# One projection moved from a mixture-of-experts routing phase into an attention phase, three routing sums in another number format, and weight splits issued in turns with gathered pieces

## The chip, the cores and the metric

The program runs on one core of a Trainium2 chip. A time is the device time of one execution of the whole program in microseconds (us); runs are compared by their median. The profiler gives the busy time of each engine: TensorE (PE; its weight loads are the separate row PEld), VectorE (DVE), ScalarE (ACT), GpSimd (POOL), and SyncE (SP), which only issues DMAs here. "Granted clock" (PEclk) is the share of TensorE's full clock that the chip granted: 1.00 is 2.4 GHz, 0.50 is 1.2 GHz.

## The reference

Two transformer blocks in float32 over T = 256 tokens of width D = 1024. The first block: causal attention, a convolutional feed-forward layer, a sliding-window attention with sinks (the "second attention" below), and again a feed-forward layer. The second block, cut to what matters here:

```python
def second_block(x, p, ...):
    h = _gdn_mixer(x, ...)                                  # gated delta net
    x = _layernorm(DEEPNORM_ALPHA * x + h, ln_g[i, 0], ln_b[i, 0])
    h = _hier_moe(x, ...)
    x = _layernorm(DEEPNORM_ALPHA * x + h, ln_g[i, 1], ln_b[i, 1])
    return x + sigmoid(x @ pe_w_gate[i]) * (p[i] @ pe_w_proj[i])   # p: 256 x 256

def _hier_moe(x, ...):                     # 4 groups of 8 experts
    g_logits = xt @ w_group + b_group
    g_onehot = one_hot(argmax(g_logits), 4)
    g_prob = sum(softmax(g_logits) * g_onehot, -1)
    e_logits = einsum("tge,tg->te", xt @ w_router + b_router, g_onehot)
    top_val, top_idx = top_k(e_logits, 2)
    top_w = softmax(top_val) * g_prob[:, None]
    # each expert: silu(xt @ w_gate) * (xt @ w_up), weighted, @ w_down
```

The product of `p` and `pe_w_proj` needs nothing of `x`, so it can be computed anywhere before the last line.

## The kernel before

Most weights are split into two halves: ScalarE rounds a piece of the loaded `raw` to fp32r (`whi`, L204), VectorE subtracts that from `raw` and keeps the rest (`wlo`, L207), and TensorE adds three products for each block, high by high, high by low and low by high (L217 to L219; for the experts L1350 to L1352). Some products are plain fp32 (L262, and p's), which the trace shows as two records each. Products of a projection go to PSUM tiles named `acc`.

The second attention (L770 on) runs over four chunks c of the query projection, each followed by softmax and attention for two pairs of heads: mask and scores (L445 to L449), maxima on VectorE (L451), exponentials on ScalarE (L463, into `pr`), transposes of the probabilities (L489), products with the values (L497).

The second block's mixture of experts has two phases. `d1` is the routing. `token_norm` makes the 36 logits `lg` (4 of groups, 32 of experts) from products that were formed along with the delta net's output projection (`rt`), the mean and rsqrt of the variance. `tokens` transposes x to token-major (`xtr`, `xt`) and makes its high half `xth` and the full normalized `xt`; `tokens_low` the low half `xtl`. `route` makes the one-hot group `g1h`, sums it over tokens on TensorE (`pp`, L1232 to L1236, with constant matrices `below` and `ones`), and from it the place of each token in its group (`key`); `put` makes the 0/1 matrices `kept` that sort tokens by group. `by_slot` gathers the sorted tokens with products (`ga`, L1291) and makes high and low halves of eight pieces (`xgh` on ScalarE L1304; `full` L1306 and `xgl` L1307 on VectorE); half 0 serves the first two groups. `over` looks whether a group has too many tokens (`ov`, the last reader of `pp`) and `weigh` computes the weights of the top two experts (up to `wi`). `side` is p's projection: 32 records `ppp` (L1432) in fp32, copied by ScalarE to `kept` tiles (L1433), which stay until the last line of the block.

`d2` runs over 4 groups of 8 experts. For each expert there are 24 products of gate and up (`gu`), an activation and a gate (`sg`, L1356, L1357, with the combining weight `cb`), a transposition (`htr`, L1363) and the down products (`y`, L1379 to L1381). Parts of other work run between them (`aside`: the combining weights `cbp` and `cb`, layer norm, the gather's second half).

Loads go through SyncE's queue into a ring of eight `raw` tiles in the second block (three in the attention phase); five pairs of `whi` and `wlo` hold split pieces of 1024 columns, four pieces being one expert's gate and up. Pools give a buffer out again when its last reader is done. The order on each engine is made by a scheduler; `behind(...)` says that instructions are issued after a given one. Each engine runs its list in order.

## Time and profile before

| | us |
|---|---|
| median of 3 runs (lowest and highest) | 1313.37 (1313.19 to 1313.55) |
| profiled execution | 1312.89 |
| its span | 1311.1 |
| TensorE busy | 1278.9 (98%) |
| VectorE busy | 1019.1 (78%) |
| ScalarE busy | 790.2 (60%) |

All times in this text are on the axis of the profiled execution's span, which begins at 0. The second attention's four chunks lie between 343.5 and 399, the routing phase between about 961 and 982, the experts behind it until 1240.

A line of the timeline names the start, the duration, the engine, the source line, what is written from what, the shape, and in brackets the time for which the engine stood idle ahead of it and what it waited for. Lines of source are those of the kernel before.

### The profile page before, as it was taken

The page shows a single profiled execution, that of the slowest core. Times are in us where ns is not written, and L with a number is a line of the kernel's source. Part 1 is how long each engine was busy: PE and PEld are TensorE (multiplying, and loading weights), DVE is VectorE, ACT ScalarE, POOL GpSimd, SP SyncE. Part 2 cuts the span into 40 slices and gives each one's busy share as a digit, 9 for nine tenths or more (in the row PEclk, how much of TensorE's full clock was granted, in tenths as well). Part 3 has the DMA queues.
Part 4 walks back from the last instruction along what each step waited for, and adds up shares of the span by engine and source line. Part 5 has one row for each costly group of instructions (what it writes and reads, how often), then busy time and mean ns, then how long its engine had stood idle before and what let it go on. Part 6 is the DMA issues. An engine that isn't in the chain of part 4 may idle for free.

```text
span 1311.1 us, 26079 instructions
## 1 busy us (share of the span) xinstructions
PE 1278.9 (98%) x10092; PEld 1149.3 (88%) x10092; DVE 1019.1 (78%) x2215; ACT 790.2 (60%) x1628; POOL 28.5 (2%) x51
## 2 busy tenths in 40 slices
PE   7999999999999999999999999999999999999998
PEld 7888999999879999999888787888987888888877
DVE  6677989866788988755766888666368899999985
ACT  6555667755556677653434464644257887878763
POOL 1000000000000010000100000000000000000000
PEclk9999999999999999999999999999989999999999
DMA  7434555555423555662254323243437999999951
GB/s 285 143 101 139 180 187 176 177 190 177 156 97 130 173 193 184 225 215 79 97 152 126 100 60 102 66 134 99 170 130 288 360 340 354 365 358 376 347 192 35
DMA packets 69570, 244.50 MB, mean 186 GB/s; under 512 B 24128, under 2 KB 26176, under 8 KB 45632
## 3 DMA queue, kind: packets, MB, share of 16 engines
q1 hardware_dynamic: 68288, 241.26, 52.9%
q8 instruction: 81, 1.33, 0.4%
q10 hardware_dynamic: 1152, 1.51, 0.4%
q14 instruction: 49, 0.40, 0.1%
HBM read 240.12 MB, written 2.62 MB: 185 GB/s over the span
## 4 chain that ended last, share of the span: by engine, by line
PE 86%; DVE 9%; ACT 2%; issue 1%; DMA 1%; SPq 0%; DVEq 0%; ACTq 0%
PE acc L217 11%; PE acc L218 11%; PE acc L219 11%; PE acc L292 10%; PE gu L1351 4%; PE gu L1350 4%; PE gu L1352 4%; PE acc L262 4%; PE y L1379 2%; PE y L1380 2%; PE y L1381 2%; PE acc L1614 2%; PE o L1164 2%; DVE wlo L207 1%; PE sc L489 1%
## 5 line engine op out<-in xcount | busy, mean ns | idle before, releaser
L207 DVE TENSOR_TENSOR wlo<-raw,whi 128x512 fp32r<-128x512 f32 (+1 forms) x542 | 467.8, 878 | 102.4 <-ACT whi L204 98.2
L204 ACT ACTIVATE whi<-raw 128x512 fp32r<-128x512 f32 (+1 forms) x542 | 418.1, 780 | 191.9 <-PE acc L218 132.7
L217 PE MATMUL acc<-xh,whi 128*128 128x256 f32 x892 | 258.0, 290 | 0.0
L219 PE MATMUL acc<-xh,wlo 128*128 128x256 f32 x892 | 252.0, 283 | 0.0
L218 PE MATMUL acc<-xl,whi 128*128 128x256 f32 x892 | 251.0, 282 | 0.0
L219 PEld LDWEIGHTS acc<-xh,wlo 128*128 128x128 f32 x892 | 169.8, 190 | 2.5 <-issue 2.5
L217 PEld LDWEIGHTS acc<-xh,whi 128*128 128x128 f32 x892 | 167.7, 188 | 3.0 <-issue 1.5
L218 PEld LDWEIGHTS acc<-xl,whi 128*128 128x128 f32 x892 | 168.0, 188 | 2.5 <-issue 1.5
L292 PE MATMUL acc<-x,raw 128*128 128x256 f32 x640 | 154.0, 386 | 0.4 <-issue 0.4
L292 PEld LDWEIGHTS acc<-x,raw 128*128 128x128 f32 x640 | 116.4, 190 | 15.0 <-issue 0.8
L1351 PE MATMUL gu<-wlo,xgh 128*128 128x512 f32 x256 | 103.7, 405 | 0.0
L1352 PE MATMUL gu<-whi,xgl 128*128 128x512 f32 x256 | 101.0, 394 | 1.7 <-DVE xgl L1307 1.6
L1350 PE MATMUL gu<-whi,xgh 128*128 128x512 f32 x256 | 101.3, 396 | 0.0
L219 PE MATMUL acc<-hh,wlo 128*128 128x256 f32 x352 | 99.6, 283 | 0.0
L218 PE MATMUL acc<-hl,whi 128*128 128x256 f32 x352 | 99.6, 283 | 0.0
L217 PE MATMUL acc<-hh,whi 128*128 128x256 f32 x352 | 99.6, 283 | 0.0
L262 PE MATMUL acc<-xf,raw 128*128 128x256 f32 x296 | 71.3, 379 | 0.0
L217 PEld LDWEIGHTS acc<-hh,whi 128*128 128x128 f32 x352 | 67.6, 192 | 0.0
L219 PEld LDWEIGHTS acc<-hh,wlo 128*128 128x128 f32 x352 | 67.6, 192 | 0.0
L218 PEld LDWEIGHTS acc<-hl,whi 128*128 128x128 f32 x352 | 67.6, 192 | 0.0
L1352 PEld LDWEIGHTS gu<-whi,xgl 128*128 128x128 f32 x256 | 48.6, 190 | 12.2 <-DVE xgl L1307 3.4
L262 PEld LDWEIGHTS acc<-xf,raw 128*128 128x128 f32 x296 | 52.9, 190 | 5.6 <-issue 0.2
(423 smaller groups left out, 2290.4 us busy)
## 6 DMA issues: line engine op xcount, KB each, us to landing
raw<-w_gu SPq DMA_DIRECT2D x64, 1024.0 KB, 7.3
raw<-w_up SPq DMA_DIRECT2D x44, 1024.0 KB, 4.8
raw<-w_ed SPq DMA_DIRECT2D x32, 1024.0 KB, 7.2
raw<-w_gin SPq DMA_DIRECT2D x96, 256.0 KB, 3.3
raw<-w_down SPq DMA_DIRECT2D x16, 1024.0 KB, 4.9
raw<-w_qk SPq DMA_DIRECT2D x8, 1024.0 KB, 5.0
raw<-w_gout SPq DMA_DIRECT2D x32, 256.0 KB, 2.9
raw<-w_down SPq DMA_DIRECT2D x8, 768.0 KB, 4.3
```

What stands on the lines that cost most here:

```text
L204: B.hi = nc.scalar.activation(hi[:, :m], raw[:, a : a + m], AF.Copy)
L207: i = eng.tensor_tensor(lo[:, :m], raw[:, a : a + m], hi[:, :m].bitcast(F32), op=ALU.subtract)
L217: nc.tensor.matmul(ps, wh, ah, start=first, stop=False, skip_group_check=True)
L218: nc.tensor.matmul(ps, wh, al, start=False, stop=False, skip_group_check=True)
L219: return nc.tensor.matmul(ps, wl, ah, start=False, stop=last, skip_group_check=True)
L262: nc.tensor.matmul(ps[:, m], rv[:, k, m * P : (m + 1) * P], full.f[:, k0 + k], start=k0 + k == 0 and m == 0, stop=k0 + k == nk - 1, skip_g ...
L292: nc.tensor.matmul(ps[:, m], raw[:, k, m * P : (m + 1) * P], act(k0 + k), start=k0 + k == 0 and m == 0, stop=k0 + k == nk - 1, skip_group_ ...
L1164: nc.tensor.matmul(o[:, t, h], at[:, d, blk], u[step][:, tu, h], start=i == 0, stop=i == 2)
L1350: nc.tensor.matmul(gu, xgh[:, kg, :], hv[:, k, :], start=kg == 0, stop=False)
L1351: nc.tensor.matmul(gu, xgh[:, kg, :], lv[:, k, :], start=False, stop=False)
L1352: nc.tensor.matmul(gu, xgl[:, kg, :], hv[:, k, :], start=False, stop=kg == KD - 1)
L1379: nc.tensor.matmul(y[g][c], hh[:, j, :], hi[:, s], start=first, stop=False)
```

## The change

Four things change.

p's projection is a generator, `p_steps`, that runs one of four chunks after each chunk c of the second attention, with the accumulators and the ring of that phase. The results are written to a DRAM tile and read back by two DMAs at the start of `d1`.

In `token_norm` the logits take the mean ahead of rsqrt, so that behind it stand two operations instead of four.

The group one-hot is fp32r, as are copies of `below` and `ones` (`sum01`); three sums are formed where five were, and the two that only `over` needs move into it.

The first four splits of expert weights (the four pieces of the first expert) are issued in turns with the eight pieces of the gather's first half, two pieces behind each split; `over`, `weigh` and the last two `put` come behind all of these. The loading of the overflow flag moves into `aside`.

```diff
+    def p_steps(dst):
+        p = B.wk.tile([P, 2, T], F32, name="p", tag="xn", bufs=2)
+        nc.sync.dma_start(p, A["p"])
+        raw = B.wr.tile([P, 2048], F32, name="raw", tag="raw")
+        nc.sync.dma_start(raw, A["pe_proj"])
...
+        for c in range(4):
+            ps = B.pa.tile([P, 2, T], F32, name="acc", tag="acc")
+            for m in range(2):
+                for k in range(2):
+                    nc.tensor.matmul(ps[:, m], w[:, c, k, m], p[:, k], start=not m and not k, stop=k == 1, skip_group_check=True)
+            s = B.wk.tile([P, 2, T], F32, name="pps", tag="qk")
+            nc.scalar.activation(s, ps, AF.Copy)
+            nc.sync.dma_start(dst[:, 2 * c : 2 * c + 2], s)
+            yield
...
+        R.pp = B.dr.tile([P, KD, T], F32, name="pp")
+        aside = p_steps(R.pp)
         for c in range(4):
...
                 attend_pair(pr, both, vs[0], vs[1], out, t)
+            next(aside)
...
-        nc.vector.tensor_copy(mean, rt[:, :, 36])
+        nc.vector.tensor_scalar(mean, rt[:, :, 36], -1.0, None, op0=ALU.mult)
...
+        for t in range(2):
+            nc.vector.scalar_tensor_tensor(lg[:, t], R.row[:, 0], mean[:, t : t + 1], rt[:, t, :36], op0=ALU.mult, op1=ALU.add)
...
         r = rsqrt(v)
-        nc.vector.scalar_tensor_tensor(nm, mean, -1.0, r, op0=ALU.mult, op1=ALU.mult)
...
-            nc.vector.scalar_tensor_tensor(lg[:, t], R.row[:, 0], nm[:, t : t + 1], R.row[:, 1], op0=ALU.mult, op1=ALU.add)
-            nc.vector.scalar_tensor_tensor(lg[:, t], rt[:, t, :36], r[:, t : t + 1], lg[:, t], op0=ALU.mult, op1=ALU.add)
+            nc.vector.scalar_tensor_tensor(lg[:, t], lg[:, t], r[:, t : t + 1], R.row[:, 1], op0=ALU.mult, op1=ALU.add)
+        nc.vector.tensor_tensor(nm, mean, r, op=ALU.mult)
...
-        nc.tensor.matmul(pp[:, 0, :], con("below"), oh[:, 0, :], start=True, stop=True)
...
+        nc.tensor.matmul(pp[:, 0, :], below, ohr[:, 0, :], start=True, stop=True)
+        nc.tensor.matmul(pp[:, 1, :], ones, ohr[:, 0, :], start=True, stop=False)
+        M.mm = nc.tensor.matmul(pp[:, 1, :], below, ohr[:, 1, :], start=False, stop=True)
...
         def over():
+            for t in range(2):
+                nc.tensor.matmul(pp[:, 2, :], ones, ohr[:, t, :], start=t == 0, stop=t == 1)
...
-            for a, n1, hi, lo in wload(wgu(g, e, half), 2048):
+            for a, n1, hi, lo in first[2 * half : 2 * half + 2] if first and g == e == 0 else wload(wgu(g, e, half), 2048):
...
-                    fill = side(M, tag="pq", bufs=3)
-                    next(fill)
+                    for i in range(2):
+                        nc.sync.dma_start(M.pp[i], R.pp[:, 4 * i : 4 * i + 4])
+                        nc.scalar.activation(M.sum01[:, i], con(("below", "ones")[i]), AF.Copy)
...
-                    with behind(M.fill):
-                        for _ in by_slot(*half(0), 8, tag="ga", bufs=GA):
-                            pass
-                    with behind(M.ga, M.low):
-                        for _ in fill:
-                            pass
+                    pieces, first = chain(*(wload(A["w_gu"][0, i], 2048) for i in range(2))), []
+                    with behind(M.xf, M.low):
+                        first.append(next(pieces))
+                        slots = by_slot(*half(0), 8, tag="ga", bufs=GA)
+                        next(slots)
+                    for _ in range(3):
+                        with behind(M.slot, M.sx):
+                            first.append(next(pieces))
+                            next(slots)
+                    with behind(M.sx):
                         over()
                         weigh()
                         put(2), put(3)
```

How the order moves on the engines, at three places. First TensorE's list in the second attention, in its first chunk. Before, behind the mask products (L445) stand the plain products of the next chunk's query projection (L262) and its split ones:

```order
L445 MATMUL sc<-maskr_87,identr 128x384 x4
L262 MATMUL acc<-xf,raw 128x256 x4
L217 MATMUL acc<-xh,whi 128x256
L218 MATMUL acc<-xl,whi 128x256
L219 MATMUL acc<-xh,wlo 128x256
```

Of the change, the same place, where `acc<-p,raw` (L516) is p's projection:

```order
L445 MATMUL sc<-maskr_87,identr 128x384 x4
L516 MATMUL acc<-p,raw 128x256 x4
L262 MATMUL acc<-xf,raw 128x256 x3
L447 MATMUL sc<-k_4089,q_4215 128x128 x2
L449 MATMUL sc<-k_4089,q_4215 128x256 x2
...
L516 MATMUL acc<-p,raw 128x256
L489 MATMUL sc<-cst_74,pr 128x128 x3
L516 MATMUL acc<-p,raw 128x256 x2
L489 MATMUL sc<-cst_74,pr 128x128 x3
L516 MATMUL acc<-p,raw 128x256
L489 MATMUL sc<-cst_74,pr 128x128 x3
L497 MATMUL sc<-pts,v_4090 64x128 x6
```

Products of p's projection stand behind the mask products and between the transposes of the probabilities, and the scores stand nearer to the mask than before.

Second, VectorE's list in the routing phase, from the tokens' low half on. Before, where `ov` is the overflow's read of the sums, `wlo` a weight split, `full` and `xgl` a piece of the gather:

```order
L1223 TENSOR_TENSOR xtl<-xt,xth 128x1024 x2
L1247 TENSOR_REDUCE place<-key 128x2
L1250 TENSOR_SCALAR ov<-pp 128x4
L1259 TENSOR_TENSOR ge<-lg,fm_m 128x8
L1265 TENSOR_TENSOR es_12078<-lg,g1h 128x64
L1243 TENSOR_SCALAR kept<-cst_74,key 128x128 x4
L207 TENSOR_TENSOR wlo<-raw,whi 128x1024
L1248 TENSOR_SCALAR place<-place 128x2
```

Of the change:

```order
L1245 TENSOR_TENSOR xtl<-xt,xth 128x1024 x2
L207 TENSOR_TENSOR wlo<-raw,whi 128x1024
L1330 TENSOR_SCALAR full<-ga,ln 128x256
L1331 TENSOR_TENSOR xgl<-full,xgh 128x256
L1330 TENSOR_SCALAR full<-ga,ln 128x256
L1331 TENSOR_TENSOR xgl<-full,xgh 128x256
...
L1330 TENSOR_SCALAR full<-ga,ln 128x256
L1331 TENSOR_TENSOR xgl<-full,xgh 128x256
L1271 TENSOR_REDUCE place<-key 128x2
L1274 TENSOR_SCALAR ov<-pp 128x4
```

The read of the sums, `ov`, and all that weighs the experts has gone from the front of the splits and pieces to behind the last of the eight pieces; five splits stand between them.

Third, TensorE's list at the first expert's products, with the semaphores that an instruction waits for. Before:

```order
L1432 MATMUL ppp<-p,raw 128x256 x3
L1350 MATMUL gu<-whi,xgh 128x512 [waits DVE_49,Activation_49]
L1351 MATMUL gu<-wlo,xgh 128x512 [waits DVE_49]
L1352 MATMUL gu<-whi,xgl 128x512 [waits DVE_49]
```

Of the change:

```order
L1315 MATMUL ga<-kept,xtl 128x256 x11
L1374 MATMUL gu<-whi,xgh 128x512 [waits DVE_49,Activation_49]
L1375 MATMUL gu<-wlo,xgh 128x512
L1376 MATMUL gu<-whi,xgl 128x512
```

The first product waits for VectorE and ScalarE in both, before also the next ones for VectorE, one after the other; of the change only the first. It writes a PSUM bank that `pp` held in `d1`, so in both programs it stands behind the read `ov`.

## Rows read from the trace of the kernel before

**Rows 1.** The page: busy time, share of the span and instructions by engine.

```profile
PE 1278.9 (98%) x10092; PEld 1149.3 (88%) x10092; DVE 1019.1 (78%) x2215; ACT 790.2 (60%) x1628; POOL 28.5 (2%) x51
```

**Rows 2.** Windows: stretch, length, busy PE, PEld, DVE, ACT, POOL, PEclk, DMA share, GB/s.

```profile
343.50:399.00 55.50, 53.78 (x429) 44.60 (x428) 46.66 (x135) 32.92 (x115) 0.00 (x0) 1.00 0.29 97
965.00:972.00 7.00, 5.56 (x19) 4.94 (x19) 3.39 (x14) 4.10 (x4) 0.00 (x0) 0.50 0.00 0
994.00:996.00 2.00, 2.00 (x6) 1.59 (x5) 1.84 (x4) 1.07 (x2) 0.00 (x0) 0.50 0.96 401
1000.00:1240.00 240.00, 240.00 (x1132) 199.19 (x1131) 223.26 (x251) 193.83 (x244) 0.00 (x0) 1.00 0.96 355
```

**Rows 3.** The chain of waits, 343 to 399: start, length, what.

```profile
343.71 1.73 PE acc L262 x8
```

**Rows 4.** TensorE's waits, 343.5 to 399: waiting, waited for, total, times, longest.

```profile
PE sc L489 <- DVE pr L475: 1.5, 3, 0.8
```

**Rows 5.** The tile `ppp`: count, shortest, median and longest ns, first and last start.

```profile
L1432 PE MATMUL ppp<-p,raw x32: 378/379/774, 968.6 to 981.9; 128*128 128x256 f32 x32
L1433 ACT ACTIVATE kept<-ppp x4: 586/600/612, 972.4 to 982.5; 128x512 f32<-128x512 f32 x4
```

**Rows 6.** Timeline, 964 to 982: start, length, operation, idle time before.

```profile
964.64 0.42 DVE L838 SCALAR_TENSOR_TENSOR lg<-row,lnm 128x36 f32<-128x36 f32 x2
...
966.44 0.59 PE L1232 MATMUL pp<-g1h,cst 128*128 128x4 f32 x2 [1.46 <-DVE g1h L1202]
...
967.92 1.23 ACT L1217 ACTIVATE xt<-xt,lnm,rs_y 128x1024 f32<-128x1024 f32 x1
...
968.59 3.76 PE L1432 MATMUL ppp<-p,raw 128*128 128x256 f32 x8
...
971.79 2.75 PE L1291 MATMUL ga<-kept,xth 128*128 128x256 f32 x16
...
972.88 1.23 ACT L1217 ACTIVATE xt<-xt,lnm,rs_y 128x1024 f32<-128x1024 f32 x1
...
974.15 1.23 DVE L1223 TENSOR_TENSOR xtl<-xt,xth 128x1024 fp32r<-128x1024 f32 x1 [3.17 <-ACT xt L1217]
...
975.36 0.15 DVE L1250 TENSOR_SCALAR ov<-pp 128x4 f32<-128x4 f32 x1
...
977.87 2.35 DVE L207 TENSOR_TENSOR wlo<-raw,whi 128x1024 fp32r<-128x1024 f32 x2
...
981.49 0.53 DVE L1306 TENSOR_SCALAR full<-ga,ln 128x256 f32<-128x256 f32 x1
...
981.96 0.58 PE L1350 MATMUL gu<-whi,xgh 128*128 128x512 f32 x1
```

**Rows 7.** Windows of the tile `gu` alone, first stretch of its products.

```profile
981.00:990.05 9.05, 6.39 (x22) 3.83 (x22) 0.00 (x0) 0.00 (x0) 1.00 0.79 330
```

**Rows 8.** Timeline, 989 to 1001.

```profile
989.67 0.40 DVE L1307 TENSOR_TENSOR xgl<-full,xgh 128x256 fp32r<-128x256 f32 x1
...
991.78 1.28 ACT L1356 ACT_TABLE_LOAD   x1
...
994.01 1.05 ACT L204 ACTIVATE whi<-raw 128x1024 fp32r<-128x1024 f32 x1
...
994.57 0.48 DVE L1357 SCALAR_TENSOR_TENSOR sg<-sg,cb,gu 128x256 f32<-128x256 f32 x1
...
994.77 0.63 PE L1350 MATMUL gu<-whi,xgh 128*128 128x512 f32 x1
...
995.20 0.63 PE L1351 MATMUL gu<-wlo,xgh 128*128 128x512 f32 x1
...
997.07 0.40 PE L1350 MATMUL gu<-whi,xgh 128*128 128x512 f32 x1
...
997.30 0.40 PE L1351 MATMUL gu<-wlo,xgh 128*128 128x512 f32 x1
...
1000.32 0.38 PE L1363 MATMUL htr<-cst,sg 128*128 128x128 f32 x2
```

More of the change, by code (lines that the diff above doesn't have):

```diff
@@ L1227, in route @@
         sm = lambda name, *sh: B.wk.tile([P, 2, *sh], F32, name=name, bufs=1)
-        oh = sm("g1h", NG)
+        ohr = B.wk.tile([P, 2, NG], F32R, name="g1h", bufs=1)
+        oh = ohr.bitcast(F32)
         gl = lg[:, :, 0:NG]
-        gm = first_max(gl, NG, oh)
+        gm = first_max(gl, NG, ohr)
         pp = B.pb.tile([P, 3, NG], F32, name="pp", tag="rt", bufs=1)
-        nc.tensor.matmul(pp[:, 0, :], con("below"), oh[:, 0, :], start=True, stop=True)
-        nc.tensor.matmul(pp[:, 1, :], con("ones"), oh[:, 0, :], start=True, stop=False)
-        nc.tensor.matmul(pp[:, 1, :], con("below"), oh[:, 1, :], start=False, stop=True)
-        nc.tensor.matmul(pp[:, 2, :], con("ones"), oh[:, 0, :], start=True, stop=False)
-        M.mm = nc.tensor.matmul(pp[:, 2, :], con("ones"), oh[:, 1, :], start=False, stop=True)
+        below, ones = (M.sum01[:, i] for i in range(2))
+        nc.tensor.matmul(pp[:, 0, :], below, ohr[:, 0, :], start=True, stop=True)
+        nc.tensor.matmul(pp[:, 1, :], ones, ohr[:, 0, :], start=True, stop=False)
+        M.mm = nc.tensor.matmul(pp[:, 1, :], below, ohr[:, 1, :], start=False, stop=True)
         key = sm("key", NG)
@@ L1306, in by_slot @@
                 nc.vector.tensor_scalar(full, ps[:, j - f], g, b, op0=ALU.mult, op1=ALU.add)
[L1307 removed]
+                M.sx = nc.vector.tensor_tensor(xgl[:, j, :], full, xgh[:, j, :].bitcast(F32), op=ALU.subtract)
             yield
@@ L1325, in of_slot, with experts @@
             yield
-    def experts(n, wgu, wd, xgs, cbs, done, aside=(), first=()):
+    def experts(n, wgu, wd, xgs, cbs, done, aside=(), first=None):
         sums = lambda: [B.pb.tile([P, 512], F32, name=f"y{c}", tag=f"y{c}", bufs=B.few) for c in range(2)]
@@ L1388, in experts @@
                 gu = B.pb.tile([P, 512], F32, name="gu", tag="gu", bufs=2)
-                with behind(*first):
-                    enter(g, e, gu, 0)
-                    B.pool = 1 << 30
-                    step()
-                    h = sg and turn(*sg)
-                    enter(g, e, gu, 1)
-                first = ()
+                enter(g, e, gu, 0)
+                step()
+                h = sg and turn(*sg)
+                enter(g, e, gu, 1)
                 step()
@@ L1418, in scatter @@
             then and then(f)
-            yield
-    def side(M, **tag):
-        p = B.wk.tile([P, 2, T], F32, name="p", bufs=1)
-        nc.sync.dma_start(p, A["p"])
-        raw = B.wr.tile([P, 4, 2, 2, P], F32, name="raw", tag="raw")
-        nc.sync.dma_start(raw.rearrange("p c k m f -> p (c k m f)"), A["pe_proj"])
-        yield
-        for c in range(4):
-            ps = B.pb.tile([P, 2, T], F32, name="ppp", **tag)
-            for m in range(2):
-                for k in range(2):
-                    M.fill = nc.tensor.matmul(ps[:, m], raw[:, c, k, m], p[:, k], start=not m and not k, stop=k == 1, skip_group_check=True)
-            nc.scalar.activation(M.pp[c // 2][:, 2 * (c % 2) : 2 * (c % 2) + 2], ps, AF.Copy)
             yield
@@ L1471, in moe @@
             M.put = kept((2, NG, P), F32R)
+            M.sum01 = mp.tile([P, 2, P], F32R, name="sum01")
             M.xth = mp.tile([P, 2, D], F32R, name="xth")
@@ L1503, in moe, with flag @@
                 with phase("d2", 0):
-                    M.any = nc.values_load(M.over[0:1, 0:1], min_val=0, max_val=1)
+                    def flag():
+                        M.any = nc.values_load(M.over[0:1, 0:1], min_val=0, max_val=1)
+                        yield
                     def xgs(g):
@@ L1517, in moe @@
                     last = dict(tag="yo"), dict(tag="gu", bufs=2, then=then)
-                    aside = [of_slot(puts, M, get, cb, tag="yo"), layer_norm(x, M, tag="yo"), by_slot(*half(1), tag="yo")]
+                    aside = [of_slot(puts, M, get, cb, tag="yo"), layer_norm(x, M, tag="yo"), by_slot(*half(1), tag="yo"), flag()]
                     experts(NG, lambda g, e, h: A["w_gu"][g * NE + e, h], lambda g, e: A["w_ed"][g * NE + e], xgs,
-                            lambda g: cb[:, g], lambda g, y: scatter(x, M, y, get[:, g, :], 1.0 if g else ALPHA, **last[g == NG - 1]), aside, (M.xx, M.low))
+                            lambda g: cb[:, g], lambda g, y: scatter(x, M, y, get[:, g, :], 1.0 if g else ALPHA, **last[g == NG - 1]), aside, first)
                 embed(x, M)
```

8 lines of the change are left out of this document (3 added, 5 removed).

## The prediction

> **What bounds the kernel now.** I read the page first, then the stretches around each edit, then the single instructions there. TensorE is busy 1278.9 of the 1311.1 us of the span [rows 1], so the end is set by what TensorE must do and by the few places where it stops. The stretches [rows 2] show which kind each place of the change is. In the second attention (343.5 to 399) TensorE is busy for 53.78 of 55.5 us: full. In the routing it is not: 5.56 of 7 us from 965 to 972, at a granted clock of 0.50. From 1000 to 1240 it is busy for 240.00 of 240. So there are two questions: what a full stage pays for new work, and how late the routing hands over to the experts, since nothing idle follows there that could take a delay back.
>
> **Part 1, p's projection into the second attention.** Removed from the routing are 32 matmul records and 4 copies [rows 5]. The same sixteen fp32 products (two records each, 256 columns) stand in the second attention now. Eight such records of the query projection take 1.73 us on the chain of that stage [rows 3], 0.216 each; 32 are 6.93 us. What hides them? TensorE's idle time there is 55.5 - 53.78 = 1.7 us, and its only named wait is for softmax's probabilities, 1.5 us in three pieces [rows 4]. If new products fall exactly into these, 5.2 us are left; if none do, 6.9. The scheduler does put them ahead of transposes that wait for those probabilities, but it also puts a part of the query products ahead that stood there, so waits may open elsewhere: three such as the longest, 0.8 us, bring it to 9.3. From below, the weight loads are busy for 44.60 of 55.5 us [rows 2], and if these are the true bound the cost is nothing. I take 6, near the rows on TensorE. The four copies (0.60 each) go to ScalarE, busy for 32.92 of 55.5 us; the four stores and two loads go to SyncE's queue, in a stretch with a DMA share of 0.29: both nothing. Should the query weights queue behind them, a load comes later, but it has the other loads' slots ahead of it; I price no wait there.
>
> Only from a page: the Trainium skill ("Perfetto Trace Analysis", section Identifying the Most-Contended Engine) says that matmul busy time misleads on how near TensorE is to its limit, since matmuls are pipelined, and that the busy share of weight loads tells more. By that the stage has 10.9 us of room and the 6.93 cost nothing; the trace speaks against it as far as one wait of 1.5 us is all that it shows idle.
>
> **Part 2, the routing up to the first gather.** Behind rsqrt, four operations become two; the first pair takes 0.42 us [rows 6], so the logits come 0.4 earlier. The sums: ten records from 966.44 until the eight of ppp at 968.59, 2.15 us [rows 6], become three in fp32r. No row shows such a product with 4 columns; if time goes by records it is 0.65, so 1.5 are saved; the bounds are 0 and 2.15. They end near 967.1 then. The eight ppp records (3.76 us from 968.59) no longer stand ahead of the gather at 971.79 [rows 6], which can start near 968.0, when the high half of the tokens is there. ScalarE's second full copy starts at 972.88, behind a copy of ppp that had to wait for these records; without it that copy follows the first (967.92, 1.23 us) [rows 6] and ends near 970.4. VectorE's low half for tokens follows at 971.6 instead of 974.15 + 1.23 = 975.38. So this part gains 3.8 us, if it counts, and with what the logits and sums give, up to 4.7. The two constant copies to fp32r and two readbacks lie in front of all this and are hidden by the end of the delta net.
>
> **Part 3, splits by turns, and what the first expert waits for.** From there VectorE sets the pace: five splits at 1.18 (2.35 for two), eight pairs of 0.53 + 0.40 [rows 6]: 5.9 + 7.5 = 13.4 us. With 0.8 us for the first weights' high half and 0.2 per turn for ScalarE's half, the last low piece ends at 971.6 + 13.4 + 1.6 = 986.6, against 989.67 + 0.40 = 990.07 before [rows 8]. That is 3.5 earlier, for the weighing's small operations, which stood between them, now stand behind. But there is a wait that goes with it. The first product of the first expert takes over the PSUM bank of the sums, and waits in both programs for the last read of it, `ov`. Before, `ov` came at 975.36, ahead of the gather's pieces, and the first product ran at 981.96 [rows 6]; from there products moved along with the pieces, and 22 of 24 had run by 990.05 [rows 7]. Now `ov` stands behind all eight pairs, so none of them runs before 986.8. Queued behind that product are all of TensorE's 48 of two experts and the combining weights, and nothing fills the gap from about 974 on.
>
> At the full clock a product follows the other after 0.23 us (997.07 to 997.30), at half after 0.43 (994.77 to 995.20) [rows 8]. 24 take 5.6 us and end at 992.4; if the clock is at half for the first 4 us (before, it was at least from 994 to 996 [rows 2], and was back at 997.07), nine products run in these and 15 behind, and they end at 994.2. Then comes the chain up to the first transposed hidden tile (`htr`, 1000.32 before): all five pairs of split buffers are taken by then, so that ScalarE's next splits each wait for six products. Six products 1.4, four splits of 1.05 4.2, the table load 1.28, the last split's low half 1.2, and two activations, the copy of the combining weights and the gate, at most the gate's 0.48 each, 1.7 [rows 8]: 9.8. `htr` comes at 1002.2 to 1004.0. Before, two products (0.47) were yet to come at that point, so the lag is 1.4 to 3.2; I take 2.5. The bounds are wider: -4.7 if the earlier pieces are all that counts, and 9.6 more if all 48 products run at half clock.
>
> Since TensorE is busy for 240.00 of the next 240 us [rows 2], the lag lasts. The experts' weight loads start a few us later, as a buffer kept for p's result is freed by the delta net's last splits; their first use is 970, so nothing.
>
> **The sum.** The profiled execution took 1312.89 us, 1.8 more than its span, and 0.5 less than the median of the runs, 1313.37. 1312.9 + 6 + 2.5 = 1321.4 in the profile's terms, 1321.9 in the median's: 1322.
>
> **The rivals.**
> Hidden projection. Weight loads bound the second attention, and the 6.93 us disappear in it; the routing still loses 2.5. For it: 44.60 of 55.5. Against: 53.78. 1313.4 + 2.5 = 1315.9.
> Faster. The path through the routing was the eight ppp records and the copy that waited for them; the pieces come 3.5 to 4.7 earlier and the experts with them, since the products that had run meanwhile are caught up behind them, and the projection is hidden as well. For it: the gather stood directly behind ppp. Against: the late `ov`. 1313.4 - 4.7 = 1308.7. It is decided by `htr`: earlier than 1000.32, or not.
> No change. The routing gains these 4.7, and the second attention pays 6: 1314.7, or with 5 and less 1313.
> Half clock, slower. Before, TensorE was granted 1.2 of 2.4 GHz from 965 to 972, in a stretch of waits, and again from 994 to 996 [rows 2], after VectorE's pieces had set its pace [rows 7]. The gap from 974 to 986.8 is longer than either of these. If half clock lasts over both experts' first halves, 48 x 0.20 = 9.6 us are lost, of which 1.8 are in the bounds above: 1322 + 7.8 = 1330. It decides if the granted clock is 0.50 until past 1000. The Trainium skill ("TensorE: Matmul & The Clock Gate", Part 1) names the throttled state as the default, which only sustained work releases; the trace agrees with the order of events, 0.50 behind waits and 1.00 over the 240 us of full work.
>
> **Chances.** The forecast 0.60 (its own range 1318 to 1327), hidden projection 0.09, faster 0.12, no change 0.10, half clock 0.09. Faster or slower count beyond 0.2%, 2.6 us, about what a measurement of this kernel can tell. Faster 0.12; the same 0.10 and half of the hidden projection, which lies on the bound: 0.14; slower 0.74. For 8 times in 10 the range leaves out the faster case and some of the half clock: 1313.5 to 1329.
>
> **What would show it.** Right: TensorE's busy time between 343 and 406 larger by 6 to 7 us, and the stage longer by 5 to 7; the sums 1.5 us shorter, the gather's first product near 968; no expert product before the last low piece near 986.6, a wait of TensorE for VectorE of over 10 us; `htr` at 1.4 to 3.2 us later, relative to the start of the routing. Wrong: the second attention no longer than before; an expert product between the pieces; `htr` earlier than before; or a wait for w_gu's loads behind 970.

## The result, and the profile after

The changed kernel takes 1321.88 us (median of 4 runs, 1321.33 to 1322.58), the kernel before on the same chip 1313.28 us (4 runs, 1308.02 to 1313.55). The ratio is 1.0077, 95% interval [1.0055, 1.0098]: slower by 8.6 us. The forecast was 1322.0. The total is right to 0.1 us, but not every term is: two are off by 3 to 4 us, in opposite directions.

The page of the changed kernel, busy time by engine (span 1319.9 us):

```profile
PE 1276.4 (97%) x10087; PEld 1147.4 (87%) x10087; DVE 1021.7 (77%) x2215; ACT 790.8 (60%) x1630; POOL 29.0 (2%) x51
```

TensorE is busy for 2.5 us less than in [rows 1], in a span that is 8.8 us longer: what was added as work was also taken away as work. TensorE is idle for 11.3 us more, and more of its busy time runs at half clock.

To see where the 8.8 us arose I compare starts of the same instruction in both traces. At the 181st weight split (`wlo`, ahead of the second attention's chunks) the changed kernel is at 334.87, the old one at 335.22: -0.35. At the 217th (behind these chunks): 441.27 against 434.83, +6.44. At the 325th: +6.45. At the routing's first transposition (`xtr`): 964.36 against 961.90, only +2.46; so the delta net gave back 4.0. At the fifth expert's first `htr` record: 1041.99 against 1034.59, +7.40. At the 541st split, near the experts' end: +8.32. By stage:

| stage | before | after | difference | forecast |
|---|---|---|---|---|
| second attention (181st to 217th split) | 99.61 | 106.40 | +6.8 | +6 |
| delta net (325th split to `xtr`) | 366.85 | 362.85 | -4.0 | 0 |
| routing and first experts (`xtr` to fifth expert's `htr`) | 72.69 | 77.63 | +4.9 | +2.5, with the row below |
| the other experts (to the 541st split) | 230.05 | 230.97 | +0.9 | |

Most of the last row is no loss but work that crossed the mark between the last two rows: of the sixteen `xn` records (the layer norm that runs between the experts), four stand behind the fifth expert's `htr` (1041.99) in the changed kernel and none before (1034.59). They are 0.60 us of TensorE. The tile `xn` before and after (count, shortest, median and longest ns, first and last start):

```profile
L1443 PE MATMUL xn<-cst,xt x16: 270/272/273, 1015.9 to 1029.9; 128*128 128x128 f32 x16
```

```profile
L1449 PE MATMUL xn<-cst,xt x16: 270/272/273, 1026.7 to 1042.5; 128*128 128x128 f32 x16
```

Windows of the changed kernel, columns as in [rows 2]: the second attention, the gap in the routing, two stretches of experts' products, and the experts behind them:

```profile
343.15:405.45 62.30, 60.60 (x469) 49.54 (x468) 49.04 (x140) 37.93 (x124) 0.00 (x0) 1.00 0.35 119
974.40:988.00 13.60, 1.14 (x10) 0.94 (x8) 12.23 (x25) 7.96 (x12) 0.00 (x0) 0.72 0.37 121
988.15:993.80 5.65, 5.65 (x13) 4.43 (x14) 4.68 (x28) 1.43 (x4) 0.00 (x0) 0.50 0.17 70
1006.30:1011.00 4.70, 4.70 (x13) 3.79 (x13) 1.08 (x3) 1.82 (x3) 0.00 (x0) 0.50 0.45 190
1015.00:1245.00 230.00, 229.98 (x1082) 190.50 (x1082) 213.83 (x241) 184.12 (x231) 0.00 (x0) 1.00 0.96 356
```

The second attention is as full as before (60.60 of 62.30 us), only longer. In the gap TensorE has 1.14 us of work in 13.6. Both stretches behind it run at a granted clock of 0.50.

TensorE's waits in the second attention and in the routing (waiting, waited for, total, times, longest), and p's records in their new place:

```profile
PE sc L489 <- DVE pr L475: 1.5, 4, 0.4
```

```profile
PE gu L1374 <- DVE ge L1283: 12.6, 1, 12.6
...
PE ptr L1347 <- DVE cb L1342: 2.0, 1, 2.0
```

```profile
L516 PE MATMUL acc<-p,raw x32: 377/379/382, 343.3 to 386.6; 128*128 128x256 f32 x32
```

The waits for the probabilities are 1.5 us again, as in [rows 4], in four pieces for three: the 32 records, 0.38 us each in the trace and 0.216 apart, hid in nothing. In the routing the long wait is the one that the forecast named; the profile puts it down to `ge`, which stands on VectorE directly behind `ov`. The run `over_early` below decides between the two: with `ov` early and `ge` as late as here, the wait is gone. The timeline of the routing, in the order of [rows 6] and [rows 8]:

```profile
968.46 0.24 PE L1256 MATMUL pp<-g1h,sum 128*128 128x4 f32 x1 [2.11 <-DVE g1h L1224]
...
968.67 0.25 PE L1258 MATMUL pp<-g1h,sum 128*128 128x4 f32 x1
968.96 0.17 DVE L1260 SCALAR_TENSOR_TENSOR key<-pp,g1h 128x8 f32<-128x8 f32 x1 [0.65 <-PE pp L1258]
...
969.98 3.51 PE L1315 MATMUL ga<-kept,xth 128*128 128x256 f32 x16 [0.42 <-ACT xth L1237]
...
987.44 0.42 DVE L1331 TENSOR_TENSOR xgl<-full,xgh 128x256 fp32r<-128x256 f32 x1
...
987.86 0.15 DVE L1274 TENSOR_SCALAR ov<-pp 128x4 f32<-128x4 f32 x1
...
988.15 0.77 PE L1374 MATMUL gu<-whi,xgh 128*128 128x512 f32 x1 [12.61 <-DVE ge L1283]
...
990.00 0.63 PE L1375 MATMUL gu<-wlo,xgh 128*128 128x512 f32 x1
...
990.42 0.63 PE L1376 MATMUL gu<-whi,xgl 128*128 128x512 f32 x1
...
994.22 0.40 PE L1376 MATMUL gu<-whi,xgl 128*128 128x512 f32 x1
...
1001.98 1.85 PE L1340 MATMUL cbp<-wi,kept 128*128 128x8 f32 x16
...
1003.18 2.44 DVE L207 TENSOR_TENSOR wlo<-raw,whi 128x1024 fp32r<-128x1024 f32 x2 [1.42 <-ACT whi L204]
...
1005.54 0.18 DVE L1342 COPY cb<-cbp 128x32 f32<-128x32 f32 x1
...
1005.78 0.69 PE L1347 MATMUL ptr<-cst,kept 128*128 128x128 f32 x2 [1.96 <-DVE cb L1342]
...
1006.30 0.69 PE L1387 MATMUL htr<-cst,sg 128*128 128x128 f32 x2
...
1007.22 0.63 PE L1375 MATMUL gu<-wlo,xgh 128*128 128x512 f32 x1
...
1007.64 0.63 PE L1376 MATMUL gu<-whi,xgl 128*128 128x512 f32 x1
```

The sums are 0.1 us apart now (three from 968.46 to 968.67) and `key` follows 0.5 us behind the first. Before it came 2.33 us behind the first (966.44 to 968.77):

```profile
968.77 0.17 DVE L1238 SCALAR_TENSOR_TENSOR key<-pp,g1h 128x8 f32<-128x8 f32 x1 [2.39 <-PE pp L1236]
```

The gather starts at 969.98, the last low piece ends at 987.86, and in that same microsecond `ov` and the first expert's product run. That product's followers are 0.43 apart, at half clock. Then comes a second gap: the copy `cb` stands behind two low halves of splits, TensorE waits 1.96 us for it, and after sixteen narrow products and this wait the clock is at half again (1007.22 to 1007.64: 0.42).

In the delta net, TensorE's stops for which the profile shows no cause ("issue") and the window behind the longest one, first of the kernel before:

```profile
PE wp L1059 <- issue: 1.6, 1, 1.6
```

```profile
897.80:901.20 3.40, 3.40 (x18) 3.40 (x17) 0.69 (x1) 0.63 (x1) 0.00 (x0) 0.50 0.00 0
```

Of the kernel after, and of the kernel `shift` below:

```profile
PE vp L1116 <- issue: 1.1, 1, 1.1
...
PE wp L1113 <- issue: 0.6, 1, 0.6
```

```profile
PE vp L1099 <- issue: 1.1, 1, 1.1
...
PE wp L1096 <- issue: 0.4, 1, 0.4
```

Before, a stop of 1.6 us at L1059 was followed by 3.4 us at half clock, which costs 1.7 by an estimate (half of a full stretch). After the change the stops sit at other instructions and no half clock follows. What TensorE waits for at these stops is shown under `shift`.

### The profile page after: what moved, and what is told of

It reads as the page before. It is cut to its first block, busy times and chain, and to the rows that moved or that the text cites. A ratio compares the mean times of both kernels' runs of the same rounds, so it can differ in the third digit from the quotient of the medians.

```text
span 1319.9 us, 26080 instructions
## 1 busy us (share of the span) xinstructions
PE 1276.4 (97%) x10087; PEld 1147.4 (87%) x10087; DVE 1021.7 (77%) x2215; ACT 790.8 (60%) x1630; POOL 29.0 (2%) x51
## 4 chain that ended last, share of the span: by engine, by line
PE 87%; DVE 8%; ACT 3%; issue 1%; DMA 0%; SPq 0%; DVEq 0%; ACTq 0%
PE acc L219 11%; PE acc L218 11%; PE acc L217 11%; PE acc L292 11%; PE gu L1374 5%; PE gu L1375 4%; PE gu L1376 4%; PE acc L262 4%; PE y L1403 2%; PE y L1404 2%; PE y L1405 2%; PE acc L1626 2%; PE o L1186 2%; DVE wlo L207 1%; PE sc L489 1%
## 5 line engine op out<-in xcount | busy, mean ns | idle before, releaser
L207 DVE TENSOR_TENSOR wlo<-raw,whi 128x512 fp32r<-128x512 f32 (+1 forms) x542 | 468.8, 877 | 106.4 <-ACT whi L204 101.8
L1374 PE MATMUL gu<-whi,xgh 128*128 128x512 f32 x256 | 102.9, 402 | 12.6 <-DVE ge L1283 12.6
L219 PE MATMUL acc<-hh,wlo 128*128 128x256 f32 x352 | 99.6, 283 | 0.0
L218 PE MATMUL acc<-hl,whi 128*128 128x256 f32 x352 | 99.6, 283 | 0.0
L217 PE MATMUL acc<-hh,whi 128*128 128x256 f32 x352 | 99.6, 283 | 0.0
L262 PE MATMUL acc<-xf,raw 128*128 128x256 f32 x296 | 72.6, 382 | 0.0
L1374 PEld LDWEIGHTS gu<-whi,xgh 128*128 128x128 f32 x256 | 49.3, 193 | 23.5 <-issue 12.8
L218 PEld LDWEIGHTS acc<-hl,whi 128*128 128x128 f32 x352 | 67.6, 192 | 0.0
L219 PEld LDWEIGHTS acc<-hh,wlo 128*128 128x128 f32 x352 | 67.6, 192 | 0.0
L217 PEld LDWEIGHTS acc<-hh,whi 128*128 128x128 f32 x352 | 67.6, 192 | 0.0
L262 PEld LDWEIGHTS acc<-xf,raw 128*128 128x128 f32 x296 | 52.6, 189 | 7.5 <-issue 2.2
```

Of the source, the lines that this page charges most:

```text
L207: i = eng.tensor_tensor(lo[:, :m], raw[:, a : a + m], hi[:, :m].bitcast(F32), op=ALU.subtract)
L217: nc.tensor.matmul(ps, wh, ah, start=first, stop=False, skip_group_check=True)
L218: nc.tensor.matmul(ps, wh, al, start=False, stop=False, skip_group_check=True)
L219: return nc.tensor.matmul(ps, wl, ah, start=False, stop=last, skip_group_check=True)
L262: nc.tensor.matmul(ps[:, m], rv[:, k, m * P : (m + 1) * P], full.f[:, k0 + k], start=k0 + k == 0 and m == 0, stop=k0 + k == nk - 1, skip_g ...
L1374: nc.tensor.matmul(gu, xgh[:, kg, :], hv[:, k, :], start=kg == 0, stop=False)
```

## The experiments

The measure for the routing is the stretch from `xtr` to the fifth expert's first `htr`, in one profiled execution each. "Delta net" and "second attention" are the stages of the table above. All runs of one group shared a chip with the kernel before (median 1311.98 for the first four, 1312.68 for the next four, 1312.97 for the last three). The kernel before ranges from 1307.5 to 1316.2 in these runs, so that differences of 2 us between medians are read from the stages, not from the medians. The profiled execution is not always a typical one: that of `both` (1312.12) is the fastest of its ten, that of `weigh_early` (1316.96) lies 1.8 above its median.

| kernel | second attention | delta net | routing | median us | ratio to before |
|---|---|---|---|---|---|
| before | 99.6 | 366.9 | 72.7 | | |
| after | 106.4 | 362.9 | 77.6 | 1321.88 | 1.0077 [1.0055, 1.0098] |
| p_only | 106.4 | 362.8 | 67.6 | 1311.91 | 0.9996 [0.9980, 1.0013] |
| over_early | 106.4 | 362.9 | 73.0 | 1317.43 | 1.0046 [1.0031, 1.0061] |
| p_back | 99.7 | 367.8 | 73.0 | 1316.34 | 1.0017 [1.0000, 1.0034] |
| both | 99.7 | 365.0 | 72.5 | 1314.82 | 1.0025 [1.0008, 1.0043] |
| no_turns | 106.5 | 362.9 | 66.6 | 1310.99 | 0.9994 [0.9981, 1.0007] |
| weigh_early | 106.5 | 364.9 | 71.2 | 1315.18 | 1.0027 [1.0013, 1.0040] |
| turns_kept | 106.3 | 362.9 | 69.8 | 1315.07 | 1.0022 [1.0005, 1.0039] |
| shift | 101.9 | 362.9 | 71.4 | 1316.97 | 1.0037 [1.0024, 1.0049] |
| sums_only | 99.8 | 366.8 | 70.3 | 1311.89 | 0.9990 [0.9977, 1.0004] |
| late_only | 99.8 | 367.4 | 70.5 | 1311.33 | 0.9991 [0.9977, 1.0005] |
| p_late | 99.7 | 364.9 | 70.8 | 1308.26 | 0.9969 [0.9958, 0.9981] |

Behind the stretch called routing, the experts up to the 541st split take 230.05 us in eight of these traces and 230.9 to 231.0 in `after`, `over_early`, `p_back`, `both` and `turns_kept`, the five in which four `xn` records stand behind the mark. Between a kernel of the one kind and one of the other, the loss at the experts' end is 0.9 us more than the routing column says.

**p_only: p's projection moved, nothing else.**

```diff
 (to the kernel before)
+        aside = p_steps(R.pp)
...
+            next(aside)
...
-                    fill = side(M, tag="pq", bufs=3)
...
+                        nc.sync.dma_start(M.pp[i], R.pp[:, 4 * i : 4 * i + 4])
```

> The kernel before with one part of the change alone: p's projection in the second attention and through memory; sums, logits, splits and the overflow's read of the sums as before, no p records left in the routing. Theory A (the routing lost because the overflow's read of the sums came behind all pieces): the second attention is 6 to 7 us longer, TensorE has no wait of 12 us in the routing, and from the logits to the last transposed hidden tile it takes no longer than before (304.3 us), perhaps 4 less. 1313.4 + 6.8 - 4 to 0 = 1316 to 1320. Rival B (it lost because p's records no longer keep TensorE busy there and its clock falls): these stretches are as long as with the whole change, 310 us, and the time is near 1322. Apart from both, the delta net may be 4 us shorter than before, as with the whole change, if its stop of TensorE hangs on where the code stands.

The second attention is 6.8 longer, the routing 5.1 shorter, with no fill in it. Rival B is out as a cause by itself: without the late read, the lack of p's records costs the routing nothing (with it, it does: see `p_back`). On the contrary, their going is worth 5.1 us there, and with the delta net's 4.0 pays for the second attention. Theory A has the cause, but its 1316 to 1320 was missed: 1311.91 is 4 below it, as the routing gained more than the 4 us allowed for and the delta net the 4.0 that the sum left out.

**over_early: the overflow's read moved to the front.**

```diff
 (to the kernel after)
                         put(0), put(1)
+                    with behind(M.pt):
+                        over()
...
                     with behind(M.sx):
-                        over()
                         weigh()
```

> The whole change, but the overflow's sums and their read stand directly behind the first two matrices of places, ahead of the splits and pieces. Theory A: the wait of 12.6 us is gone, the first expert's products begin near 976 to 978 and go along with the pieces, the first transposed hidden tile comes 31 to 36 us behind the logits instead of 39.4, and the time falls by 4 to 9 us, to 1313 to 1318. Rival B (lack of p's records, clock): the products begin earlier but at half clock for most of the way, and the time stays within 2 us of 1321.9. Rival C (the splits by turns set the pace): the last low piece stays at 987.9 and the tile at 39 us behind the logits.

TensorE's products at the first expert and its waits in the routing, of this kernel:

```profile
977.56 0.39 PE L1374 MATMUL gu<-whi,xgh 128*128 128x512 f32 x1
977.79 0.40 PE L1375 MATMUL gu<-wlo,xgh 128*128 128x512 f32 x1
```

```profile
PE gu L1376 <- DVE xgl L1331: 3.0, 7, 1.4
PE ptr L1347 <- DVE cb L1342: 2.7, 1, 2.7
PE gu L1375 <- DVE wlo L207: 1.7, 4, 0.8
```

The wait of 12.6 us is gone, the first product runs at 977.56, at full clock, and the routing is 4.7 shorter: theory A. Its sizes came at the weak end: `htr` 35.6 us behind the logits (968.3 to 1003.90) for 31 to 36, and 4.5 us of time for 4 to 9. 73.0 is still 5.4 more than with p moved alone. Two things are left in the rows, 4.7 us of waits for pieces and splits and 2.7 for `cb`.

**p_back and both: p's projection behind the gather, with the late and with the early read.**

```diff
 (to the kernel after, without p_steps and the two readbacks)
+                    fill = side(M, tag="pq", bufs=3)
...
+                    with behind(M.ga):
+                        for _ in fill:
+                            pass
                     with behind(M.sx):
```

> The whole change, but p's projection is back in the routing, all of it behind the gather's products; nothing of it in the second attention or memory. Theory A: the second attention is 6 to 7 us shorter again, TensorE still waits for the late read of the sums but has p's 7 us of work in the gap, so that its clock is lower for a shorter time: 1321.9 - 6.8 - 0 to 3 = 1312 to 1315. Rival C: ScalarE's four copies of 0.6 us stand between the pieces and make the last one 2.4 us later, 1315 to 1317.

> The whole change with both edits: p's projection behind the gather's products in the routing, and the overflow's read of the sums ahead of the splits and pieces. What is left of the change are the logits, the fp32r sums and the splits by turns. Theory A: both gains add, 1321.9 - 6.8 - 4 to 9 = 1306 to 1311, faster than before. Rivals B and C: one of the two gains is the other again, 1313 or more.

The second attention is back at 99.7 in both, so these 6.8 us belong to p's records. In `p_back` the routing takes 73.0 for 77.6, a gain of 4.6 where 0 to 3 were expected, but the delta net of its profiled execution takes 367.8 for 362.9, which is why that one is at 1316 and not at 1312. Its ten times lie in two groups, four from 1312.0 to 1313.1 and six from 1316.3 to 1317.0, so that the 4.9 us need not be in each. Rival C gave the right time for a wrong reason: the last low piece ends 24.2 us behind `xtr` (988.46 less 964.25), 0.7 later than after the change and not 2.4. TensorE still waits for the late read, 5.1 us instead of 12.6, and here the profile names `ov` itself:

```profile
PE gu L1354 <- DVE ov L1254: 5.1, 1, 5.1
```

With the early read on top (`both`) the routing is only 0.5 shorter still. The two gains are one: p's 7 us fill the gap that the late read makes. Theory A's sum for `both`, 1306 to 1311, is missed by that and by a delta net of 365.0; rivals B and C, 1313 or more, have the time right.

**weigh_early, turns_kept and no_turns: the weighing, and the turns.** In `weigh_early` the weighing is issued behind the first turn; in `turns_kept` also the combining weights' products one step later; `no_turns` is the whole change without its last part.

```diff
 (weigh_early, to over_early)
                         next(slots)
+                    with behind(M.low):
+                        weigh()
...
                     with behind(M.sx):
-                        weigh()
                         put(2), put(3)
...
 (turns_kept, to weigh_early)
-                    aside = [of_slot(puts, M, get, cb, tag="yo"), ...
+                    aside = [iter((0,)), of_slot(puts, M, get, cb, tag="yo"), ...
```

> The whole change, with the overflow's read early as before and also the weighing of the experts issued behind the first turn, so that its small operations stand between the pieces; the splits still come by turns. Theory A2 (what was left to lose with the early read, 5.4 us against p's projection moved alone, is that the combining weights come behind all pieces): the stretch falls from 73.0 to 67 to 69 us, the time from 1317.4 to 1312 to 1314. Rival E (the splits by turns themselves cost it): it stays at 72 us or more.

> As the kernel with the early read and the early weighing, but the products for the combining weights are issued one step later, behind the first expert's 24 products; in that kernel they stood ahead of nine of them and TensorE waited 4.1 and 1.2 us for the weights. What differs from the change without splits by turns is then the turns alone. Theory A3 (of the 11.0 us between 77.6 and 66.6 us, all comes from where the overflow's read and the weighing stand, none from the turns): the stretch from the routing's first transposition to the fifth expert's hidden tile is 66 to 68 us, the time 1311 to 1313. Rival E (the turns cost something of their own, since ScalarE's and VectorE's halves of a piece wait for each other): 70 us or more, 1314 or more.

> The whole change without its last part: p's projection in the second attention, early mean in the logits, fp32r sums; the splits, the gather's pieces, the overflow's read and the weighing stand as in the kernel before. The measure is the stretch from the routing's first transposition to the fifth expert's hidden tile: 72.7 us before, 77.6 with the whole change, 73.0 with the early read of the sums, 67.6 with p's projection moved alone. Theory A2 (splits by turns and all that stands behind the pieces cost what p's removal gained): 66 to 67 us, and a time of 1309 to 1312. Rival D (the early logits or fp32r sums do harm, for instance by the clock): 70 us or more, 1314 or more.

TensorE's waits in the routing of `weigh_early`, and the whole stretch of `turns_kept`, then of `no_turns`, as windows:

```profile
PE cbp L1340 <- DVE wi L1306: 4.1, 1, 4.1
PE cbp L1340 <- DVE kept L1265: 1.2, 1, 1.2
```

```profile
965.67:1035.48 69.81, 62.51 (x280) 49.87 (x280) 59.11 (x122) 53.21 (x73) 0.00 (x0) 0.90 0.65 241
```

```profile
965.27:1031.85 66.58, 58.14 (x284) 48.27 (x284) 58.20 (x122) 54.01 (x75) 0.00 (x0) 0.92 0.69 256
```

`weigh_early` missed its 67 to 69, by a new wait: the combining weights' products were put ahead of nine of the first expert's and stood there for 5.3 us. `turns_kept` is without that wait, at 69.8 us. `no_turns` has 66.6 and 1310.99 us, as theory A2 had it, so rival D is out: the early logits and the fp32r sums do no harm. Taken out in this order, the 11.0 us between the whole change and the change without turns are: the late read 4.7 (77.6 to 73.0), the late weighing 3.2 (73.0 to 69.8), the turns 3.2 (69.8 to 66.6). The last step is not the turns alone: the last two `put` stand behind the pieces and the overflow flag's loading in `aside` with it, and the four `xn` records make it 4.1 at the experts' end. Theory A3 falls; rival E is right but for 0.2 us in its bound. How the turns cost 3.2 is not settled: TensorE is idle for 7.3 us with them and for 8.4 without; what grew is the time in which it counts as busy, 62.5 against 58.1, at a granted clock of 0.90 against 0.92 over the stretch. By these clocks half clock lasted about 14.0 and 10.7 us (twice 0.10 of 69.81 and twice 0.08 of 66.58), so that an estimated 1.7 of the 3.2 us is clock.

**sums_only, late_only and p_late: what a part is worth alone.** The first has the early logits and five fp32r sums ahead of the gather, the second all of p's records behind the gather's products, the third both.

```diff
 (late_only, to the kernel before)
-                    with behind(M.mm):
-                        next(fill)
                     tokens_low(M)
-                    with behind(M.fill):
+                    with behind(M.mm):
                         for _ in by_slot(*half(0), 8, tag="ga", bufs=GA):
```

> The kernel before with the early mean in the logits and the fp32r sums alone, all five ahead of the gather; p's projection stays in the routing with its first eight records ahead of the gather. Theory: sums and logits are 2.2 us shorter, and the stretch falls from 72.7 to 70.5 us, the time by 2 us. Rival: the pieces wait for p's eight records and ScalarE's copy anyway, and the stretch stays at 72 to 73 us.

> The kernel before with one edit: all 32 records of p's projection behind the gather's products instead of eight ahead of them. Theory: the gather starts 3 us earlier, the pieces too, and the stretch falls from 72.7 to 70 to 71 us. Rival: the first expert starts later behind the records, the pieces wait for nothing less, and it stays at 72 to 73 us.

> The kernel before with the early mean in the logits and the fp32r sums (all of them ahead of the gather), and with p's projection still in the routing, but all 32 records behind the gather's products, none ahead of them; no splits by turns. Theory A2: the stretch is 67 to 69 us (p's 7 us run while TensorE waits for pieces anyway), nothing is added to the second attention: 1313.3 or 1312.0 (before, on the two chips) - 4 to 6 = 1306 to 1308, faster than both kernels. Rival H (the first expert then starts 4 us later and cannot catch up): the stretch is 71 us or more, and the time that of before.

The whole stretch of `sums_only`, then of `p_late`, as windows:

```profile
962.56:1032.89 70.33, 65.02 (x316) 53.03 (x316) 58.39 (x122) 56.09 (x79) 0.00 (x0) 0.95 0.65 245
```

```profile
960.01:1030.78 70.77, 67.84 (x316) 56.33 (x316) 58.33 (x122) 56.30 (x79) 0.00 (x0) 0.91 0.66 242
```

Both alone do in the routing what was expected, -2.4 and -2.2. Together they give -1.9 and miss the 67 to 69: they don't add. `p_late` ran this stretch at a granted clock of 0.91, `sums_only` at 0.95, worth an estimated 2.8 us (0.09 of 70.77 less 0.05 of 70.33); whether that comes with the order or with the execution, one trace of each can't tell. Nor are p's records free behind the gather: `late_only` takes 70.5 us where `p_only`, with none of them, takes 67.6, and `p_late` 70.8 where `no_turns` takes 66.6. Their medians alone can't be told from the kernel before. `p_late` is faster than both kernels, by 0.3% [0.2, 0.4], but as its routing is no shorter than that of the other two, some 2 us of its gain in the traces lie in its delta net (364.9), whose length no edit aimed at.

**shift: sixteen tiny products more in the second attention.**

```diff
 (to the kernel before, once for each of the four chunks)
+            ps = B.pa.tile([P, 2, T], F32, name="acc", tag="acc")
+            for k in range(4):
+                nc.tensor.matmul(ps[:, 0, 0:2], ident, ident[:, 0:2], start=k == 0, stop=k == 3, skip_group_check=True)
+            z = B.wk.tile([P, 2], F32, name="shift", tag="shift")
+            nc.scalar.activation(z, ps[:, 0, 0:2], AF.Copy)
```

> The kernel before with sixteen more fp32 products of 2 columns in the second attention (their sums are copied and not used), as many instructions as p's projection puts there, but almost without work: TensorE's code behind it stands as far along as with the change. Theory F (TensorE's stops in the delta net hang on where its code stands): the delta net, from its first split to the routing's first transposition, takes 362.8 to 363 us as in all kernels with p moved, instead of 365 to 368; the second attention costs about 2 us. Rival G (it is chance from run to run, or p's loads late in the delta net do it): 365 to 368 us.

Its p's loads still come late in the delta net, its projection is in the routing, yet its delta net takes 362.9 us and its stops are at the same instructions as after the change [the rows above]: theory F has the place of the stops. Five of the six other kernels with p's products moved have 362.8 to 362.9 as well, the sixth 364.9; the five with p in the routing and the kernel before have 364.9 to 367.8.

What TensorE waits for there, the waits do not name, but the records of the transfers do. Of the kernel before: the stop at L1059, the queue for instructions from 894.2 to 895.2, up to the start of the stop, and the same queue over the whole span (packets, MB, share of the DMA engines):

```profile
896.69 0.75 PE L1059 MATMUL wp<-pr,z 32*32 32x16 f32 x67 [1.56 <-issue]
```

```profile
q8 instruction: 1, 0.02, 5.5%
```

```profile
q8 instruction: 81, 1.33, 0.4%
```

This one packet, of 16 KB, runs from 894.34 to 895.21, and TensorE goes on 1.47 us behind its end. The 13 traces have 31 stops of over 0.15 us without a named cause between 40 and 1290 us, all in the delta net; each ends 1.2 to 1.6 us behind the end of such a packet. A time taken at random from 600 to 960 us does so in 4 of 100 cases. There is one packet for about 250 of TensorE's 20184 products and weight loads. I read this as TensorE waiting for its code, so that with more code ahead other instructions are hit; no run changed these transfers alone.

The place is not all of the 4.0 us. `both` and `p_late`, with the old place and no half clock behind the stop, have 364.9; `before` and `sums_only` have one stretch of 3.4 us at half clock there and 366.8, `late_only` and `p_back` one of 6.8 and 367.4 and 367.8. So some 2 us go with the place, and the other 2 or 3 with half clock, which kernels with the same code up to there have or have not. With the new place only `weigh_early` has it, 3.4 us behind a stop of 1.7. Rival G's chance is not excluded for that part.

Nor is `shift` faster for it: its median is 4.3 us above the kernel before. Its trace is 4.3 us later at the 181st split, ahead of the edit, and 2.1 us longer from the 217th to the 325th, behind it, both stages that no edit touches. The stage from the 217th to the 325th split before, then in `shift`:

```profile
434.83:595.05 160.22, 160.22 (x1329) 159.38 (x1328) 128.08 (x250) 103.78 (x199) 4.71 (x4) 1.00 0.56 195
```

```profile
441.41:603.71 162.30, 162.30 (x1330) 161.47 (x1329) 128.13 (x250) 105.13 (x199) 4.72 (x4) 1.00 0.56 192
```

TensorE is busy all the time, at full clock, with the same products, and takes 1.3% longer; in the other eleven kernels this stage takes 160.2 as before. The cause is open. The second attention's 2.3 us in `shift` are therefore no price of 32 small records, since stages without them grew as well.

## Why the prediction was right, and where it was not

**Part 1** was right: 6.8 for 6, between 5.2 and 9.3, and nearer to the case in which nothing is hidden. The rival by the weight loads is out: their share was 0.80 of the stage and is 49.54 of 62.30 us, 0.80 again, so that none of the room that they seem to leave was used. The 0.80 did not say what the stage could take.

**Part 2** was right in its steps. With the 2.46 us by which the changed kernel enters the routing later taken off, `key` comes at 966.50 for 968.77 and the gather at 967.52 (forecast 968.0). The sums with the logits gave 2.3 us (forecast 1.9). Part of that is clock, which the forecast did not count: its 2.15 us for the old ten records was read at a granted clock of 0.50 (965 to 972, [rows 2]). In `p_only` the same ten records ran at full clock and took 1.1 us:

```profile
970.79 0.39 PE L1252 MATMUL pp<-g1h,cst 128*128 128x4 f32 x2 [0.93 <-DVE g1h L1222]
971.03 0.36 PE L1253 MATMUL pp<-g1h,cst 128*128 128x4 f32 x2
```

```profile
970.79:971.90 1.11, 1.11 (x10) 1.11 (x10) 0.00 (x0) 1.11 (x2) 0.00 (x0) 1.00 0.00 0
```

There `key` comes 1.0 us earlier behind `xtr` than before (5.86 for 6.87), with neither the sums nor the logits changed.

**Part 3** was right in the cause and its chain. Again less 2.46: the last low piece ends at 985.4 (forecast 986.6), the first product runs at 985.7 (986.8), the second expert's first product starts at 994.1 (forecast for the end of the first 992.4 to 994.2), `htr` comes at 1003.8 (1002.2 to 1004.0). The wait is 12.6 us (over 10).

At `htr` the forecast still held. It comes 3.5 us later than before, with two products (0.47 us) more already done, which is a lag of 3.0 us in the forecast's own count (1.4 to 3.2).

What failed is the sentence "the lag lasts". It grew. The forecast counted one spell of half clock of 4 us, in the first expert's products; there were two, of at least 5.65 and 4.7 us, the second behind `htr`, where it expected a full TensorE. 4.7 us at half clock cost an estimated 2.4, and the lag of 3.0 became 5.9 at the experts' end (4.9 at the fifth expert, where four `xn` records were still to come). The term was 2.5. The half clock rival is out all the same: it asked for 0.50 until past 1000, and the first spell was over when products took 0.40 us again, from 994.2 on.

The delta net, -4.0, was no term at all: the forecast took every stage that it did not name as unchanged. Without that gain the time would have been near 1326. So the 0.1 us by which the total was met is an accident of +0.8, +3.4, -4.0 and less than 1 us at the two ends; the direction and the two mechanisms are not.

The faster rival named its point, `htr` before 1000.32, and the point decided against it. Yet `p_only` and `no_turns` show that its mechanism exists: with the early read and without turns, p's removal does carry to the experts, 5.1 us and, with sums and logits, 6.1.

## What to carry to other kernels

When a scheduler puts a small operation behind a long series, look who waits for it: here a read of 0.15 us that freed a PSUM bank, moved behind eight pieces, held up 24 products for 12.6 us. Of work in a gap, ask what its removal and its new place each cost. In the routing p's 32 records cost 5.1 us, of which 2.2 were the eight ahead of the gather; the rest, behind it, was not free either (2.9). In a stage that is 97% busy they cost their full length, 6.8. Before two engines are made to take turns, try the old order with the other parts of the change: here the parts were worth 6 us in the routing and the turns, with what they displaced, cost 11. Where parts of a change interact, as the late read and the filling work do here, the price of a part depends on which others are in.

## What the runs showed of the hardware

TensorE's stops without a named cause go with the arrival of its code: in 13 traces all 31, of 0.2 to 1.7 us, ended 1.2 to 1.6 us behind a 16 KB packet of the queue for instructions. Sixteen products more ahead of it moved these stops in the delta net to other instructions (1.6 us at L1059 before, 1.1 us at another after), and that stage took 362.9 for 366.9 us; some 2 us of this go with half clock, which did not follow there. A stage that no edit touches can change by this much, in either direction.

Half clock came without a long gap: a wait of 1.96 us behind sixteen products of 8 columns was followed by 4.7 us at 0.50, a stop of 1.6 us by 3.4.

An fp32r product of 4 columns is 0.1 us from the next at full clock. An fp32 one takes two records and 0.23 us at full clock (970.79 to 971.03 in `p_only`), 0.43 at half clock (ten records in 2.15 us before).
